# Channel tiles of the S5 heads ahead of the second half's token part, mixers' transfers issued by GpSimd, in a two-layer hybrid decoder trunk

## The chip, the core and the metric

One Trainium2 chip, one core. The engines are TensorE (PE), VectorE (DVE), ScalarE (ACT), GpSimd (POOL) and SyncE (SP); each works through its own stream of instructions in order, and streams meet at semaphores. A transfer is issued by one of the engines and carried out by the DMA engines. The metric is the device time of one execution in microseconds; a kernel's figure is the median of its runs.

## What is computed

Two layers over 1024 tokens of width 1024. In each layer one input projection feeds three kinds of heads, their normalised outputs are joined by an output projection, and then come a feed-forward block and a gate on a per-layer input embedding `p`:

```python
def hybrid_layer(h, p_i, cos, sin, ...):
    xn = rmsnorm(h, attn_norm_g)
    z = xn @ w_in
    za, zq, zk, zv, zc = jnp.split(z, [...], axis=-1)
    ya = chunk_gmlp(za, gmlp_ln_g, gmlp_ln_b, gmlp_ws, gmlp_bs)
    q = apply_rope(rmsnorm(q, q_norm_g), cos, sin)
    k = apply_rope(rmsnorm(k, k_norm_g), cos, sin)
    yb = swa_sink_attention(q, k, v, sinks)
    yc = s5_ssm(zc, ...)
    y = jnp.concatenate([rmsnorm(ya, ...), rmsnorm(yb, ...), rmsnorm(yc, ...)], axis=-1)
    h = h + y @ w_out
    hn = rmsnorm(h, mlp_norm_g)
    h = h + jnp.square(jax.nn.relu(hn @ w_ff1)) @ w_ff2
    gate = jax.nn.sigmoid(rmsnorm(h, ple_norm_g) @ w_ple_gate)
    return h + gate * (p_i @ w_ple_proj)
```

## The kernel before

**Tiling.** The tokens are cut into two halves of 512 (`h` = 0, 1). Every fp32 product is three fp32r matmuls of high and low parts, so a weight tile is loaded (`st`), rounded by ScalarE (line 104) and its remainder taken by VectorE (line 105) before TensorE uses it. PSUM has banks by tag: two `mm`, two `s`, and one each of `p`, `o`, `x`, `t`. An accumulation group of 24 matmuls of 512 columns fills a bank.

**First phase (to about 300 us).** `project0` makes layer 0's input projection for both halves. `z_tok(l, h, part)` has tokens on partitions: part 0 gives gmlp's gate half, k and v (stored to DRAM as `zg`), part 1 gives q (`zq`); each is 96 matmuls into four banks and four evictions, in which ScalarE writes a `z` tile from pool `zs` (two buffers) and a transfer stores it. `z_chan(l, h, m)` has channels on partitions: tiles m = 0, 1 feed S5 (`zu`), 2, 3 gmlp (`za`). Before, the order is z_tok of half 0 (part 0, 1), of half 1 (part 1 with the kept weights, then part 0), then the eight channel tiles. `embed` transposes `p` and multiplies it by `w_ple_proj` for both layers; its tiles `ptk` and `pjz` come from `zs` too, and `pjz` is stored as `pj`. Beside that, `ssm_tables` and `ssm_prep` compute S5's rotation tables (`tc_`, `ts_`, by doubling) and kernels (`kt`, `gq`, `pe`), stored as `par1`, `par2`, which `ssm` loads as `p1`, `p2` with `u` from `zu`. `psS` in the trace is S5's matmul of states (line 845), `pk`, `pq` and `pss` are attention's transposes and scores.

**Main phase.** `mix_out(0, 0)` is the output projection of half 0 (input tiles 0, 1 from gmlp, 2 to 5 attention, 6, 7 S5; its first three output tiles are begun on six input tiles). Then four `window`s run (feed-forward, gate), with the mixers of the following half as side lanes: `left_lane` carries S5 and attention of both halves of layer 0, `mix_lane` those of layer 1. Lanes are generators that are advanced at rates, with flags between them (`wait`); the scheduler sets the final order of each engine's stream from the program so written.

**Queues.** Before, all 855 transfers are issued by SP, weights and mixers' loads and stores in one stream, in order. POOL computes the rotation tables (36 operations, `cmul` with the engine `self.G`), clears `xp`, and does a few set-up instructions.

Of the kernel before, what the change touches and what calls it, by code (L numbers as in the profile page):

```python
# [62 lines left out]
class Trunk:  # L63


    def __init__(self, tc, ctx, a):
        self.tc, self.ctx, self.a = tc, ctx, a
        self.nc = nc = tc.nc
        self.V, self.S, self.G, self.T, self.Q = nc.vector, nc.scalar, nc.gpsimd, nc.tensor, nc.sync
        self.lanes, self.nbank, self.flags = [], 0, set()  # L70
        self.X, self.R, self.H, self.hst = {}, {}, {}, {}

# [290 lines left out]
    def setup(self):  # L363
# [4 lines left out]
        self.zs = self.pool(self.ctx, "zs", 2)  # L368
        self.xy = self.pool(self.ctx, "xy")
# [134 lines left out]
    def ssm_tables(self, t):  # L504
# [6 lines left out]
        for i, nm in enumerate(("ssm_a_re", "ssm_a_im")):  # L511
            Q.dma_start(rows[0:N, i, :], a[nm].rearrange("l (j e) p -> (l j) (e p)", e=2))
        Q.dma_start(ldr, a["ssm_log_dt"].rearrange("l (j e) -> (l j) e", e=2))
# [76 lines left out]
        for n in (1, 2, 4, 8, 16, 32):  # L590
# [3 lines left out]
                      bc(tc_), bc(ts_), tq[:, :, 0:n], self.G)  # L594
        for l in range(DEPTH):
            for gh in range(2):
                c = slice(l * 8 + gh * 4, l * 8 + gh * 4 + 4)
                for i, x in enumerate((tc_, ts_, r0)):
                    Q.dma_start(self.par1[l][gh][:, 1024 + i * 260:1284 + i * 260],
                                x[:, c, :].rearrange("p j b -> p (j b)"))  # L600

    def ssm_prep(self, l, t, tag, nb):

        a, V, S, G, T, Q = self.a, self.V, self.S, self.G, self.T, self.Q
        for gh in range(2):
# [3 lines left out]
            for x, nm in ((br, "ssm_b_re"), (bi, "ssm_b_im")):  # L609
                Q.dma_start(x, a[nm][l, gh * 8:gh * 8 + 8].rearrange("(j e) p h -> (e p) j h", e=2))  # L610
# [9 lines left out]
            for x, nm in ((cr, "ssm_c_re"), (ci, "ssm_c_im")):  # L620
                cl = t.tile([P, 2, 64], F32, name="cl", bufs=2)
                src = a[nm][l, gh * 8:gh * 8 + 8].rearrange("g h p -> (g h) p")
                Q.dma_start(cl[:, 0, :], src)
                Q.dma_start(cl[:, 1, :], src)
# [22 lines left out]
            Q.dma_start(self.par1[l][gh][:, 0:1024], pe.rearrange("p r j c -> p (r j c)"))  # L647
# [4 lines left out]
            for ri in range(2):  # L652
                Q.dma_start(self.par2[l][gh][:, ri * 512:(ri + 1) * 512].rearrange("p (j c) -> p j c", j=4),
# [5 lines left out]
            Q.dma_start(dk, a["ssm_d"][l, gh * 8:gh * 8 + 8].rearrange("(j e) h -> (e h) j", e=2))  # L659
# [25 lines left out]
    def z_tok(self, l, h, part, weights, ss):  # L685
# [13 lines left out]
        pss = [self.bank(tag) for tag in ("s", "s", "p", "o")]  # L699
# [13 lines left out]

    def z_sums(self):
# [36 lines left out]
    def project0(self):  # L751
# [18 lines left out]
        self.z_roots(0, 1, ss)  # L770
# [8 lines left out]
    def embed(self):  # L779
# [21 lines left out]
        for l in range(DEPTH):  # L801
            for i in range(2):
                w = F.next()
                for n in range(8):
                    h, m = n // 4, n % 4
                    ps, z = self.bank("mm"), self.zs.tile([P, 512], F32, tag="z", name="pjz")
# [3 lines left out]
                    Q.dma_start(self.pj[l][h][4 * i + m], z)  # L810
# [7 lines left out]
    def ssm(self, l, h, side, tag="p"):  # L818
# [706 lines left out]
```

## Time and profile before

| | |
|---|---|
| runs | 2393.14, 2386.28, 2385.95 us |
| median | 2386.28 us |
| profiled execution, its own time | 2391.88 us |
| its span | 2390.2 us |
| PE busy | 2327.5 us (97%) |
| VectorE, ScalarE, GpSimd busy | 1551.3, 1029.1, 33.5 us |
| granted clock over the span | 0.989 |
| transfers | 294.07 MB, 41.0% of 16 DMA engines |

PE is the engine on which the time stands, so the profile is read for PE's gaps: where they lie, what released PE after each, and what that releaser was waiting for in its turn. The granted clock is a share of TensorE's full 2.4 GHz.

### The profile page before, as it was taken

The numbers are of one execution on the slowest core, as the hardware profiler recorded it, in microseconds if no ns is written. First come the engines' busy times: TensorE is split into PE (matmuls) and PEld (weight loads), VectorE is DVE, ScalarE is ACT, GpSimd is POOL, SyncE is SP. The second block draws the span as 40 slices with busy tenths as digits, with TensorE's granted clock in tenths as the row PEclk, the third lists the DMA queues.
The fourth block names the chain that finished last, engine by engine and source line by source line (L and its number), as shares of the span: only waits on it lengthen the run. The fifth ranks groups of instructions, "written<-read, shape, count | busy, mean of one in ns | idle before, by whom it ended". The sixth has DMA issues, their size and how long they took to land.

```text
span 2390.2 us, 29266 instructions
## 1 busy us (share of the span) xinstructions
PE 2327.5 (97%) x10941; PEld 1885.4 (79%) x10941; DVE 1551.3 (65%) x2664; ACT 1029.1 (43%) x1787; POOL 33.5 (1%) x51
## 2 busy tenths in 40 slices
PE   7998999999999999999999999999999999999998
PEld 5777777788788887777888888777888887888887
DVE  7777678675966765576585774676757674444455
ACT  7355646433434443553342543464334343322333
POOL 0400000000000000000000000000000000000000
PEclk9999999999999999999999999999999999999999
DMA  8555542253553345324443344422534434333333
GB/s 246 175 153 171 175 127 75 80 164 100 154 154 104 110 129 144 103 71 141 128 134 115 106 136 132 137 76 80 164 105 136 123 93 137 97 92 95 96 97 98
DMA packets 403559, 295.95 MB, mean 124 GB/s; under 512 B 66668, under 2 KB 376024, under 8 KB 401624
## 3 DMA queue, kind: packets, MB, share of 16 engines
q1 hardware_dynamic: 403416, 294.07, 41.0%
q8 instruction: 86, 1.41, 0.2%
q14 instruction: 57, 0.47, 0.1%
HBM read 250.48 MB, written 43.54 MB: 123 GB/s over the span
## 4 chain that ended last, share of the span: by engine, by line
PE 82%; DMA 6%; DVE 4%; ACT 2%; issue 1%; SPq 0%; ACTq 0%; DVEq 0%
PE mm_ps L356 44%; PE x_ps L356 20%; PE s_ps L356 8%; DMA st<-in_w_in 2%; DVE w L105 2%; ACT w L104 1%; PE po L1242 1%; PE pss L1184 1%; PE p_ps L356 1%; DMA st<-in_w_out 1%; DMA pj<-pjz 1%; PE p_ps L931 1%; PE s_ps L706 1%; PE pt L1221 1%; PE psY L888 1%
## 5 line engine op out<-in xcount | busy, mean ns | idle before, releaser
L104 ACT CAST w<-st 128x1024 fp32r<-128x1024 f32 x364 | 387.4, 1067 | 844.0 <-PE mm_ps L356 438.1
L356 PE MATMUL mm_ps<-x,w 128*128 128x512 f32 x2904 | 711.3, 397 | 8.6 <-ACT pjz L809 4.1
L356 PEld LDWEIGHTS mm_ps<-x,w 128*128 128x128 f32 x2904 | 547.0, 190 | 135.4 <-issue 11.7
L105 DVE TENSOR_TENSOR w<-st,w 128x1024 fp32r<-128x1024 f32 x364 | 448.8, 1235 | 201.8 <-ACT w L104 196.1
L356 PE MATMUL mm_ps<-A,w 128*128 128x512 f32 x2016 | 500.9, 392 | 1.3 <-DVE H L1317 1.3
L356 PEld LDWEIGHTS mm_ps<-A,w 128*128 128x128 f32 x2016 | 376.0, 188 | 84.0 <-DVE H L1317 3.3
L356 PE MATMUL x_ps<-A,w 128*128 128x512 f32 x1056 | 273.5, 393 | 4.1 <-DVE H L1317 4.1
L356 PE MATMUL x_ps<-x,w 128*128 128x512 f32 x1104 | 272.0, 393 | 0.0
L356 PE MATMUL s_ps<-x,w 128*128 128x512 f32 x1056 | 251.8, 390 | 4.4 <-DVE w L105 2.7
L356 PEld LDWEIGHTS x_ps<-x,w 128*128 128x128 f32 x1104 | 205.7, 188 | 45.6 <-issue 3.4
L356 PEld LDWEIGHTS x_ps<-A,w 128*128 128x128 f32 x1056 | 196.3, 188 | 50.7 <-DVE H L1317 8.3
L356 PEld LDWEIGHTS s_ps<-x,w 128*128 128x128 f32 x1056 | 197.8, 188 | 48.6 <-DVE w L105 4.0
L1317 DVE TENSOR_TENSOR H<-H,mm_ps 128x512 f32<-128x512 f32 x168 | 113.3, 684 | 85.0 <-PE mm_ps L356 84.3
L1328 DVE SCALAR_TENSOR_TENSOR r<-mm_ps,rbc 128x512 f32<-128x512 f32 x88 | 60.7, 689 | 116.8 <-PE mm_ps L356 116.6
L706 PE MATMUL s_ps<-w,x 128*128 128x512 f32 x384 | 101.3, 403 | 3.9 <-ACT x L89 2.0
L1317 DVE TENSOR_TENSOR H<-H,x_ps 128x512 f32<-128x512 f32 x88 | 60.2, 684 | 67.8 <-PE x_ps L356 67.2
L1332 DVE TENSOR_TENSOR A<-q,A 128x512 fp32r<-128x512 f32 x128 | 87.7, 685 | 7.1 <-ACT q L1331 6.9
L706 PEld LDWEIGHTS s_ps<-w,x 128*128 128x128 f32 x384 | 73.3, 194 | 21.3 <-ACT x L89 2.4
L1330 ACT ACTIVATE A<-r 128x512 fp32r<-128x512 f32 x128 | 80.2, 626 | 6.9 <-DVE r L1328 6.9
L1331 ACT ACTIVATE q<-r 128x512 f32<-128x512 f32 x128 | 78.9, 617 | 0.0
L1207 ACT ACTIVATE pr<-pr,anm,hf 128x128 f32<-128x128 f32 x128 | 61.6, 483 | 20.1 <-DVE anm L1204 20.1
L90 DVE SCALAR_TENSOR_TENSOR x<-H,gT,x 128x512 fp32r<-128x512 f32 x80 | 57.4, 746 | 1.4 <-ACT x L89 1.4
(381 smaller groups left out, 2130.6 us busy)
## 6 DMA issues: line engine op xcount, KB each, us to landing
st<-in_w_ff SPq DMA_DIRECT2D x256, 512.0 KB, 4.1
st<-in_w_out SPq DMA_DIRECT2D x32, 512.0 KB, 4.1
st<-in_w_ple_gate SPq DMA_DIRECT2D x32, 512.0 KB, 4.1
st<-in_w_in SPq DMA_DIRECT2D x18, 512.0 KB, 4.5
p<-par SPq DMA_DIRECT2D x8, 1024.0 KB, 6.9
pj<-pjz SPq DMA_DIRECT2D x32, 256.0 KB, 2.0
H<-hs SPq DMA_DIRECT2D x4, 2048.0 KB, 8.7
pj<-pj SPq DMA_DIRECT2D x32, 256.0 KB, 3.6
```

Of the source, the lines that this page charges most:

```text
L90: self.V.scalar_tensor_tensor(lo, x, g, hi.bitcast(F32), ALU.mult, ALU.subtract)
L104: self.S.copy(hi, src)
L105: self.V.tensor_tensor(lo, src, hi.bitcast(F32), ALU.subtract)
L356: self.T.matmul(ps, w[:, i, k, c0:c0 + P], X[:, j, k, :], start=(start and n == 0), stop=(stop and n == last))
L706: T.matmul(pss[b], X[:, j, 2 * s + kk, c], w[:, i, kk, :], start=(s == 0 and kk == 0 and n == 0), stop=(s == 3 and kk == 1 and n == 2))
L888: T.matmul(psY[:, j], gqm[:, ri, j, :], xp[:, ri, j], start=(ri == 0), stop=False)
L1207: S.activation(pr[:, i], pr[:, i], AF.Exp, bias=nm[:, i:i + 1], scale=f[:, i:i + 1], accum_out=den[:, i:i + 1])
L1317: V.tensor_tensor(H[:, m], H[:, m], ps, ALU.add)
L1328: V.scalar_tensor_tensor(r, ps, 0.0, self.R[h][1], ALU.max, ALU.mult)
L1330: S.activation(A[:, 0, m], r, AF.Square)
L1331: S.activation(q, r, AF.Square)
L1332: V.tensor_tensor(A[:, 1, m], q, A.bitcast(F32)[:, 0, m], ALU.subtract)
```

## The change

It has four parts. (1) The S5 channel tiles (m = 0, 1, both halves) stand in `project0` before part 0 of half 1, the weight plan follows, and a flag `("zu", 0, 0)` lets S5 of half 0 start when they are done; `ssm` waits for `("z", l, h)` before it writes its output into X. Part 1 of half 1 goes to banks mm, mm, s, s and part 0 to p, o, s, s. (2) The rotation tables are computed by VectorE. (3) A pool `pz` adds two `z` buffers once both parts of `z_tok` are done for both halves, for `z_chan` 2, 3 and `embed`, and is closed before `mix_out(0, 0)`. gmlp and attention of half 0 start behind that point (flag `zg` in place of `zw`), and attention of half 1 waits for `("h", 0, 0)`, the end of `mix_out(0, 0)`, in place of a flag set inside it. (4) 351 transfers are issued by POOL: all loads and stores of the mixers, the stores of `z`, the loads of `ptk`, the stores of `pj`, the tables and kernels of S5. 520 stay on SP: weights, x, `hs`, `H`, the loads of `pj`, the output. The transfers of `zu` and `yt` are cut in two halves of 64 partitions, 16 more.

```diff
 def main_plan(self):
...
+        chan = self.z_chan_plan(0)
+        yield next(chan)
+        yield next(chan)
         yield from self.z_tok_plan(0, 0)
-        yield from self.z_chan_plan(0)
+        yield from chan
...
 def ssm_tables(self, t):
...
             self.cmul(tc_[:, :, n + 1:2 * n + 1], ts_[:, :, n + 1:2 * n + 1], tc_[:, :, 1:n + 1], ts_[:, :, 1:n + 1],
-                      bc(tc_), bc(ts_), tq[:, :, 0:n], self.G)
+                      bc(tc_), bc(ts_), tq[:, :, 0:n])
...
-                    Q.dma_start(self.par1[l][gh][:, 1024 + i * 260:1284 + i * 260],
+                    self.G.dma_start(self.par1[l][gh][:, 1024 + i * 260:1284 + i * 260],
...
-    def z_tok(self, l, h, part, weights, ss):
+    def z_tok(self, l, h, part, weights, ss, tags=("s", "s", "p", "o")):
...
-            z = self.zs.tile([P, 512], F32, tag="z", name="z")
+            z = self.zt()
             S.activation(z, ps, AF.Copy, scale=sc)
-            Q.dma_start((self.zq if part else self.zg)[l][h][b], z)
+            self.G.dma_start((self.zq if part else self.zg)[l][h][b], z)
...
-        pss = [self.bank(tag) for tag in ("s", "s", "p", "o")]
+        pss = [self.bank(tag) for tag in tags]
...
+    def zt(self, name="z"):
+
+        self.nz += 1
+        pools = self.zpools
+        return pools[self.nz % len(pools)].tile([P, 512], F32, tag="z", name=name)
...
 def z_chan(self, l, h, m, w, tag):
...
-            Q.dma_start(self.zu[l][h][m].rearrange("s p b -> p s b"), zv)
+            for r in (slice(0, 64), slice(64, P)):
+                self.G.dma_start(self.zu[l][h][m][:, r].rearrange("s p b -> p s b"), zv[r])
...
 def project0(self):
...
-        yield from self.z_tok(0, 1, 1, lambda s: kept[s], ss)
-        self.flags.add("zw")
-        yield
-        yield from self.z_tok(0, 1, 0, lambda s: F.next(), ss)
+        yield from self.z_tok(0, 1, 1, lambda s: kept[s], ss, ("mm", "mm", "s", "s"))
+
+        def chan(ms):
+            for m in ms:
+                w = F.next()
+                for h in range(2):
+                    yield from self.z_chan(0, h, m, w, "mm")
+
+        yield from chan((0, 1))
+        self.flags.add(("zu", 0, 0))
+        yield from self.z_tok(0, 1, 0, lambda s: F.next(), ss, ("p", "o", "s", "s"))
         self.z_roots(0, 1, ss)
-        for m in range(4):
-            w = F.next()
-            for h in range(2):
-                yield from self.z_chan(0, h, m, w, "mm")
+        self.flags.add("zg")
+        yield
+        yield from chan((2, 3))
...
 def embed(self):
...
-                    ps, z = self.bank("mm"), self.zs.tile([P, 512], F32, tag="z", name="pjz")
+                    ps, z = self.bank("mm"), self.zt("pjz")
...
-                    Q.dma_start(self.pj[l][h][4 * i + m], z)
+                    self.G.dma_start(self.pj[l][h][4 * i + m], z)
...
 def left_lane(self):
...
-        yield from self.wait(("z", 0, 0))
+        yield from self.wait(("zu", 0, 0))
         yield from self.ssm(0, 0, 1, "x")
...
-        yield from self.wait("early")
+        yield from self.wait(("h", 0, 0))
         yield from self.attention(0, 1, 1)
...
 def run(self):
...
-        self.until(lambda: "zw" in self.flags)
+        self.until(lambda: {"zg", "rotary"} <= self.flags)
         zws.close()
-        self.until(lambda: "rotary" in self.flags)
         self.lanes.remove(z0)
+        pzs = ExitStack()
+        self.zpools.append(self.pool(pzs, "pz", 2, side=self.side(0), reuse_waits="tile"))
         self.lane(self.gmlp(0, 0, 0, "x", [("attn", 0, 0)]), RATE0)
...
         self.until(lambda: {("attn", 0, 0), ("gm", 0, 0)} <= self.flags)
+        self.zpools.pop()
+        pzs.close()
```

The lines left out turn the other `Q.dma_start` of the mixers and S5's preparation into `self.G.dma_start`, and take one name for a tile.

How the streams move, at three places. First the transfers. Before, this is SP's stream where it stores the first half's q (`zq_146`) and S5's tables (`par_113` to `par_116` are `par1` of the two layers and group halves, `par_117`, `par_118` two of `par2`):

```order
L599 DMA par_113<-tc__644 128x260
...
L647 DMA par_113<-pe 128x1024
...
L599 DMA par_113<-ts__645 128x260
...
L694 DMA zq_146<-z 128x512 x2
L681 DMA par_117<-kt 16x4x128 x16
L694 DMA zq_146<-z 128x512
```

Now the same transfers in POOL's stream, from the first store of q on:

```order
L698 DMA zq_146<-z 128x512
L685 DMA par_117<-kt 16x4x128 x16
L698 DMA zq_146<-z 128x512
L603 DMA par_113<-tc__644 128x260
...
L603 DMA par_116<-ts__645 128x260
L698 DMA zq_146<-z 128x512
L657 DMA par_118<-gq 128x4x128 x2
L698 DMA zq_146<-z 128x512
L651 DMA par_114<-pe 128x1024
L685 DMA par_118<-kt 16x4x128 x16
L698 DMA zq_147<-z 128x512 x2
```

The sixteen `kt` stores moved ahead of the second store of q, eight table stores stand between the second and the third, and the second `kt` group ahead of the fifth. Farther down the same stream of POOL, up to the load of S5's input `u`:

```order
L841 MEMSET xp 128x1024
L848 DMA p_1502<-par_113 128x1804
L850 DMA p_1504<-par_117 128x2048
L698 DMA zq_147<-z 128x512 x2
L992 DMA lng<-in_gmlp_ln_g 128x256
L992 DMA lnb<-in_gmlp_ln_b 128x256
L1134 DMA q<-zq_146 128x512
L744 DMA zu_122<-z 64x8x64 x2
L744 DMA zu_124<-z 64x8x64 x2
L1134 DMA q<-zq_146 128x512
L846 DMA u<-zu_122 128x512
```

The last two stores of the second half's q now stand behind the mixers' first loads, and the load of `u` comes 72 transfers after the first store of q.

Second, PE behind part 1 of half 1 (`x_222` and `x_447` are the normalised inputs of half 0 and 1). Before, from the end of that token projection:

```order
L706 MATMUL p_ps<-w,x_447 128x512 x6
L706 MATMUL o_ps<-w,x_447 128x512 x4
L1103 MATMUL pk<-identr,kst 128x128 x4
L706 MATMUL o_ps<-w,x_447 128x512 x2
L356 MATMUL mm_ps<-x_222,w 128x512 x23
L1103 MATMUL pk<-identr,kst 128x128 x4
L356 MATMUL mm_ps<-x_222,w 128x512
L356 MATMUL mm_ps<-x_447,w 128x512 x24
L1103 MATMUL pk<-identr,kst 128x128 x4
L1171 MATMUL pq<-identr,qst 128x128 x4
L1184 MATMUL pss<-kT,qt 128x128 x8
```

Now, from the last matmuls of part 1 (banks mm, s), and its continuation at the end of part 0:

```order
L710 MATMUL mm_ps<-w,x_447 128x512 x12
L710 MATMUL s_ps<-w,x_447 128x512 x12
L710 MATMUL p_ps<-w,x_447 128x512 x6
L710 MATMUL o_ps<-w,x_447 128x512 x5
L359 MATMUL mm_ps<-x_222,w 128x512 x24
L359 MATMUL mm_ps<-x_447,w 128x512 x24
...
L710 MATMUL s_ps<-w,x_447 128x512 x24
...
L710 MATMUL s_ps<-w,x_447 128x512 x10
L1122 MATMUL pk<-identr,kst 128x128 x8
L359 MATMUL mm_ps<-x_222,w 128x512 x24
L359 MATMUL mm_ps<-x_447,w 128x512 x24
L862 MATMUL psS<-u,p_1502 64x64 x16
```

Two S5 channel tiles moved between the first eleven matmuls of part 0 and the rest, the other two stand behind it, and S5's states follow at once; attention's first transposes stand behind part 0 instead of inside it.

Third, PE at the end of `embed` and the start of `mix_out(0, 0)`. Before (`y_1996` is S5's output before its gate, `ssq` its sum of squares, `os` attention's, `va` gmlp's; `x_2068` is the embedding, `x_1992` the joined input of the output projection):

```order
L285 MATMUL t_ps<-os,onesr 128x256
L931 MATMUL x_ps<-y_1996,gw 128x512 x6
L356 MATMUL mm_ps<-x_2068,w 128x512 x12
L931 MATMUL x_ps<-y_1996,gw 128x512 x6
L356 MATMUL mm_ps<-x_2068,w 128x512 x6
L931 MATMUL x_ps<-y_1996,gw 128x512 x6
L356 MATMUL mm_ps<-x_2068,w 128x512 x12
L285 MATMUL x_ps<-ssq,onesr 128x512
L356 MATMUL mm_ps<-x_2068,w 128x512 x6
L356 MATMUL mm_ps<-x_1992,w 128x512 x36
L356 MATMUL s_ps<-x_1992,w 128x512 x18
```

Now (`x_2246` the embedding, `x_2176` the joined input):

```order
L359 MATMUL mm_ps<-x_2246,w 128x512 x4
L1261 MATMUL po<-pp,v 64x256 x2
L359 MATMUL mm_ps<-x_2246,w 128x512 x2
L1261 MATMUL po<-pc,vd 64x256 x2
L359 MATMUL mm_ps<-x_2246,w 128x512 x12
L288 MATMUL x_ps<-va,onesr 128x512
L288 MATMUL t_ps<-os,onesr 128x256
L359 MATMUL mm_ps<-x_2246,w 128x512 x18
L359 MATMUL mm_ps<-x_2176,w 128x512 x4
L359 MATMUL s_ps<-x_2176,w 128x512 x2
```

The roots of gmlp (`va`) and attention (`os`) now stand last, with 18 embedding matmuls behind them; S5's root moved up.

## Rows read from the trace of the kernel before

**Rows 1.** The page, part 4: the chain that ended last, by engine.

```profile
PE 82%; DMA 6%; DVE 4%; ACT 2%; issue 1%; SPq 0%; ACTq 0%; DVEq 0%
```

**Rows 2.** Windows: length, busy us (instructions) per engine, granted clock, DMA share, GB/s.

```profile
0.00:400.00 400.00, 360.51 (x1788) 286.89 (x1788) 294.59 (x714) 229.20 (x507) 31.54 (x49) 0.96 0.54 164
400.00:2391.00 1991.00, 1966.97 (x9154) 1598.53 (x9153) 1256.68 (x1951) 799.86 (x1282) 1.92 (x2) 1.00 0.39 116
```

**Rows 3.** Windows around gaps; columns as above: PE, PEld, DVE, ACT, POOL.

```profile
80.00:100.00 20.00, 15.65 (x68) 12.33 (x67) 11.78 (x33) 1.82 (x3) 4.93 (x4) 0.91 0.46 146
140.00:160.00 20.00, 17.18 (x77) 14.57 (x76) 15.30 (x43) 7.84 (x18) 0.00 (x0) 0.83 0.72 193
190.00:220.00 30.00, 23.41 (x177) 18.58 (x178) 25.59 (x65) 19.61 (x51) 0.00 (x0) 0.89 0.59 192
280.00:300.00 20.00, 16.29 (x58) 12.49 (x57) 9.50 (x15) 7.23 (x14) 0.00 (x0) 0.83 0.40 138
310.00:330.00 20.00, 15.96 (x69) 12.55 (x70) 18.14 (x32) 10.31 (x16) 0.00 (x0) 1.00 0.56 157
360.00:380.00 20.00, 17.39 (x87) 15.28 (x86) 16.92 (x36) 13.79 (x38) 0.00 (x0) 0.83 0.30 92
930.00:980.00 50.00, 44.56 (x191) 35.57 (x192) 30.61 (x52) 17.70 (x29) 0.00 (x0) 0.97 0.55 152
```

**Rows 4.** PE's timeline: start, length, what, in brackets idle before and releaser.

```profile
76.07 3.23 PE L706 MATMUL s_ps<-w,x 128*128 128x512 f32 x13 [0.25 <-DVE hss L697]
...
92.67 4.61 PE L706 MATMUL o_ps<-w,x 128*128 128x512 f32 x12 [4.35 <-DVE hss L697]
...
285.69 5.49 PE L356 MATMUL mm_ps<-x,w 128*128 128x512 f32 x12 [3.71 <-ACT pjz L809]
```

**Rows 5.** SP's issue timeline, 72 to 97 us: start, length, transfers issued.

```profile
72.74 0.33 SPq L694 DMA_DIRECT2D zq<-z  x1
...
82.01 0.79 SPq L599 DMA_DIRECT2D par<-tc__644  x2
...
87.97 0.95 SPq L694 DMA_DIRECT2D zq<-z  x2
89.02 7.49 SPq L681 DMA_DIRECT2D par<-kt  x16
```

**Rows 6.** ScalarE's timeline at the fourth eviction of the first half's q.

```profile
90.65 0.69 ACT L693 ACTIVATE z<-o_ps,rtm 128x512 f32<-128x512 f32 x1 [8.88 <-DMA zq<-z]
```

**Rows 7.** SP's issue timeline near the end of the embedding.

```profile
273.33 0.37 SPq L1276 DMA_DIRECT2D H<-hs  x1
```

**Rows 8.** The chain that ended last, in order of time: start, length, what.

```profile
273.92 11.06 DMA pj<-pjz
...
478.29 10.88 PE mm_ps L356 x48
```

**Rows 9.** gmlp's root in half 0: PE's first matmul, VectorE's last step.

```profile
257.60 1.02 PE L285 MATMUL x_ps<-va,onesr 128*128 128x512 f32 x2
...
271.86 1.41 DVE L90 SCALAR_TENSOR_TENSOR x<-u,gT,x 128x512 fp32r<-128x512 f32 x2
```

**Rows 10.** POOL's instructions by form: count, busy us, mean ns, idle before.

```profile
L824 POOL MEMSET xp<- 128x1024 f32 x4 | 3.8, 956 | 1506.5 <-DVE or L294 706.1 <-DVE rt L1126 489.7 <-ACT pr L1207 280.2
L256 POOL TENSOR_TENSOR tc__644<-tc__644,tq 128x512 f32<-128x512 f32 x1 | 1.6, 1638 | 0.0
...
L255 POOL TENSOR_TENSOR tq<-ts__645 128x64 f32<-128x64 f32 x1 | 1.4, 1373 | 0.1
...
L254 POOL TENSOR_TENSOR tc__644<-tc__644 128x64 f32<-128x64 f32 x1 | 0.3, 303 | 0.0
```

**Rows 11.** Transfers by issue: engine, count, KB each, median us to landing.

```profile
zq<-z SPq DMA_DIRECT2D x16, 256.0 KB, 2.1
...
u<-zu SPq DMA_DIRECT2D x8, 256.0 KB, 3.5
```

**Rows 12.** VectorE's timeline: a product of 512 elements a row.

```profile
54.61 0.69 DVE L254 TENSOR_TENSOR pw<-lr,bbr 128x512 f32<-128x512 f32 x1
```

More of the change, by code (lines that the diff above doesn't have):

```diff
@@ L69, in __init__ @@
         self.V, self.S, self.G, self.T, self.Q = nc.vector, nc.scalar, nc.gpsimd, nc.tensor, nc.sync
-        self.lanes, self.nbank, self.flags = [], 0, set()
+        self.lanes, self.nbank, self.nz, self.flags = [], 0, 0, set()
         self.X, self.R, self.H, self.hst = {}, {}, {}, {}
@@ L368, in setup @@
         self.zs = self.pool(self.ctx, "zs", 2)
+        self.zpools = [self.zs]
         self.xy = self.pool(self.ctx, "xy")
@@ L511, in ssm_tables @@
         for i, nm in enumerate(("ssm_a_re", "ssm_a_im")):
-            Q.dma_start(rows[0:N, i, :], a[nm].rearrange("l (j e) p -> (l j) (e p)", e=2))
-        Q.dma_start(ldr, a["ssm_log_dt"].rearrange("l (j e) -> (l j) e", e=2))
+            self.G.dma_start(rows[0:N, i, :], a[nm].rearrange("l (j e) p -> (l j) (e p)", e=2))
+        self.G.dma_start(ldr, a["ssm_log_dt"].rearrange("l (j e) -> (l j) e", e=2))
         yield
@@ L622, in ssm_prep @@
                 src = a[nm][l, gh * 8:gh * 8 + 8].rearrange("g h p -> (g h) p")
-                Q.dma_start(cl[:, 0, :], src)
-                Q.dma_start(cl[:, 1, :], src)
+                self.G.dma_start(cl[:, 0, :], src)
+                self.G.dma_start(cl[:, 1, :], src)
                 pc = self.ps.tile([P, 512], F32, tag=tag, name="pc")
@@ L726, in z_chan @@
         V, Q, bc = self.V, self.Q, self.R[h][1]
-        ps, z = self.bank(tag), self.zs.tile([P, 512], F32, tag="z", name="z")
+        ps, z = self.bank(tag), self.zt()
         yield from self.cm(ps, w, 0, self.X[h], range(NK))
@@ L787, in embed @@
                 for b in range(2):
-                    t = self.zs.tile([P, 512], F32, tag="z", name="ptk")
+                    t = self.zt("ptk")
                     r = (4 * h + 2 * b) * P
-                    Q.dma_start(t.rearrange("p (b c) -> p b c", b=2),
+                    self.G.dma_start(t.rearrange("p (b c) -> p b c", b=2),
                                 a["p"][l, 0, r:r + 2 * P, :].rearrange("(b p) c -> p b c", p=P))
@@ L828, in load @@
             u = sp.tile([P, 8, 64], F32, name="u")
-            Q.dma_start(u.rearrange("p g b -> p (g b)"), zu[gh].rearrange("s (h g) b -> (s h) (g b)", g=8))
+            self.G.dma_start(u.rearrange("p g b -> p (g b)"), zu[gh].rearrange("s (h g) b -> (s h) (g b)", g=8))
             p1 = sp.tile([P, 1804], F32, name="p1")
-            Q.dma_start(p1, self.par1[l][gh])
+            self.G.dma_start(p1, self.par1[l][gh])
             p2 = sp.tile([P, 2048], F32, name="p2")
-            Q.dma_start(p2, self.par2[l][gh])
+            self.G.dma_start(p2, self.par2[l][gh])
             st[gh] = [u, p1, p2]
@@ L891, in outputs @@
             S.copy(ye, psY)
-            Q.dma_start(yu[gh].rearrange("t (h g) b -> (t h) (g b)", g=8), ye.rearrange("p j e b -> p (j e b)"))
+            self.G.dma_start(yu[gh].rearrange("t (h g) b -> (t h) (g b)", g=8), ye.rearrange("p j e b -> p (j e b)"))
             yt = sp.tile([P, 512], F32, tag="yt", name="yt")
-            Q.dma_start(yt.rearrange("p (t b) -> p t b", t=8), yu[gh].rearrange("t p b -> p t b"))
+            for r in (slice(0, 64), slice(64, P)):
+                self.G.dma_start(yt[r].rearrange("p (t b) -> p t b", t=8), yu[gh][:, r].rearrange("t p b -> p t b"))
             st[gh].append(yt)
@@ L944, in ssm @@
         yield
+        yield from self.wait(("z", l, h))
         X = self.X[h]
@@ L961, in gmlp @@
         va = gm.tile([P, 4, 256], F32, name="va")
[L962 removed]
+        self.G.dma_start(va, self.zg[l][h][:, :, 0:256].rearrange("b p c -> p b c"))
         u = gm.tile([P, 2, 512], F32, name="u")
[L964 removed]
+        self.G.dma_start(u, self.za[l][h])
         wl = gm.tile([P, 4, P], F32, name="wl")
[L966 removed]
+        self.G.dma_start(wl, a["gmlp_ws"][l].rearrange("a p c -> p a c"))
         bsb = gm.tile([P, 2, P], F32, name="bsb")
         for hh in range(4):
[L969 removed]
+            self.G.dma_start(bsb[(hh % 2) * 64:(hh % 2) * 64 + 64, hh // 2, :], a["gmlp_bs"][l, hh].partition_broadcast(64))
         lng = gm.tile([P, 256], F32, name="lng")
@@ L972, in gmlp @@
         for x, nm in ((lng, "gmlp_ln_g"), (lnb, "gmlp_ln_b")):
[L973 removed]
+            self.G.dma_start(x, a[nm][l].rearrange("a b -> (a b)").partition_broadcast(P))
         yield
@@ L1285, in mix_out @@
             yield from self.wait(("ssm", l, h))
-            self.flags.add("early")
         for m in range(NK):
```

29 lines of the change are left out of this document (12 added, 17 removed).

## The prediction

> **What bounds the kernel now.** I began with the chain of waits [rows 1]: TensorE (PE) makes 82% of the chain that ended last, so a change that leaves its matmuls as they are (and this one does) can only move the gaps between them and the clock. The windows say where the gaps are [rows 2]: in the first 400 us PE is busy 360.51, so 39.5 us are idle at a mean clock of 0.96; in the 1991 us behind, 24.0 are idle at 1.00. More than half of what can be won lies in the first sixth of the span, which is where the change is. A finer table [rows 3] has the spots: idle us, plus the length times what the clock lacks of 1.00. They are 80 to 100 (4.35 + 1.8 = 6.2), 140 to 160 (2.8 + 3.4 = 6.2), 190 to 220 (6.6 + 3.3 = 9.9), 280 to 300 (3.7 + 3.4 = 7.1), 310 to 330 (4.0), 360 to 380 (2.6 + 3.4 = 6.0), 930 to 980 (5.4 + 1.5 = 6.9): 46.3 in all. Where the clock falls, PE had a gap just before: the 4.35 us gap ends at 92.67 [rows 4], and the window around it has 0.91.
>
> Then the queue of transfers on SyncE (SP), because two of the gaps end there. At 80 to 100 [rows 5] the first eviction store zq<-z leaves at 72.74, but the next two only at 87.97, behind eight transfers of the rotation tables that GpSimd (POOL) is computing until then, the first of which leave at 82.01. ScalarE (ACT), with two z buffers, sits 8.88 us before its next eviction [rows 6], and PE waits for the o bank. At 273.33 the 2 MB load H<-hs is issued [rows 7], a store pj<-pjz behind it takes 11.06 us on the chain [rows 8], and PE waits 3.71 us for pjz at 285.69 [rows 4].
>
> **The change part by part.** The sum is made against the profiled execution (2391.88 us, span 2390.2), which lies 5.6 us above the median of 2386.28; I carry that difference unchanged and subtract from the median. About 0.3%, 7.2 us, is what a measurement of this kernel tells from no change.
>
> Gains. (1) 80 to 100: the stores no longer stand behind transfers that wait for the tables, and the second half's first part uses banks mm, mm, s, s, so PE doesn't need the o bank there. I take 6 of 6.2. (2) 140 to 160: attention started amid token projection; by the order it now starts behind it, with channel tiles beside it. I take 5 of 6.2, since the waits for kT and qt are its own. (3) 190 to 220 and 280 to 300, embedding: four z buffers instead of two let a load or store be two tiles late, and the stores pj<-pjz leave the queue that carries H and the weights. I take 14 of 17.0. (4) 310 to 330: the waits here are casts and the residual sum; weights are freer on SP. 2 of 4.0. (5) 360 to 380, second half's attention: the softmax chain stays. 3 of 6.0. (6) 930 to 980, with weight loads on SP no longer behind mixers' loads: 4 of 6.9. Sum 34; the bounds are 0 and 46.3.
>
> Cost 1, the end of the first phase. Before, S5's root came last and 54 early matmuls of the output projection followed it. Now gmlp's root is last, with 18 embedding matmuls behind it, and the output projection's first input tile is gmlp's. From that root's matmul (257.60) to the end of the tiles that it yields (271.86 + 1.41) took 15.7 us [rows 9]. A 512-column matmul takes 10.88/48 = 0.227 us [rows 8], so 18 of them cover 4.1; 11.6 are bare, and I add 3.4 us of clock, the loss beside the 3.71 us gap (280 to 300). 15.0 us. From below it is 0 if lanes run sooner than the order suggests.
>
> Cost 2, GpSimd as issuer. 351 transfers move to it, in one queue in a fixed order. No row of before shows what it takes GpSimd to issue one. SP took 7.49/16 = 0.47 us for a kt store [rows 5], the cheap end; GpSimd's dearest instruction was 1.64 us [rows 10], the dear end. I take 0.956 us, its memset: an instruction that reads no tensor, as a descriptor list does not, though it is far from the same thing. Call the price p. By the order, behind the first zq store (at about 76, where PE starts the second half, [rows 4]) stand 16 kt stores, zq store 2, eight table stores, zq store 3 (26th), store 4 (29th), 16 more kt stores, store 5 (47th), and as the 72nd the load of u. With two z buffers, eviction n waits for store n-2. PE starts the second half at 76.07; 96 matmuls and some 2 us of small ones end at about 100; after 11 more it wants the mm bank of eviction 5 (102.5), after 48 + 13 more the s bank of eviction 7 (116.4), after 72 more, the k transposes (1.1) and 48 more the states' u (144.7). A store lands in 2.1 us, u in 3.5 [rows 11], an eviction is 0.69 [rows 6]. Lateness: mm 26p - 23.7, s 47p - 37.6, u (with the memset of 0.96) 72p - 64.2. At 0.47 all are negative: nothing. At 0.956 they are 1.2, 7.3 and 4.6, and the largest counts: 7.3 us. At 1.64 it is 53.9. Behind that come loads with slack: at 0.956 the queue is idle most of the time (351 x 0.956 = 336 of 2390 us).
>
> The Trainium skill (SBUF — State Buffer, section "SBUF: two separate sides") speaks against this move: descriptors of a GpSimd-issued transfer are written by GpSimd itself, and while VectorE holds the port pair that the two share they can't be; it gives about 620 ns alone and 3100 ns beside a copy on VectorE. By 3.1 us cost 2 would be, as an estimate, 72 x 3.1 - 64.2 = 159 us. No run here shows a transfer from GpSimd.
>
> Tables on VectorE: 36 operations, from 512 elements a row (0.69 us, [rows 12]) down to 16, about 10 us in all. VectorE has 105 us free in the first 400 [rows 2], so I take 0; without that cover at most 10. Split zu and yt transfers, 16 more issues: in p. Reordered weights: the two S5 tiles need their weights earlier, and the same casts run. 0.
>
> Sum: 34 - 15.0 - 7.3 = 11.7 us; 2386.3 - 11.7 = 2374.6, say 2375.
>
> **The rivals.** (a) GpSimd's queue becomes the bound, slower. Mechanism: in-order issue from 76 to 165 us holds z buffers, then banks, then u. Nothing else changed, it pays from cost 2 = 19.2, that is p = 1.16 (72p = 83.4); slower by over 0.3% from p = 1.26. Speaking for it: GpSimd's instructions stretch while VectorE works; two products of the same 64 elements took 303 and 1373 ns [rows 10], and VectorE is busy 74% of the first 400 us [rows 2]. A mean of 1.45 gives 40.2 us, 2386.3 - 34 + 15 + 40.2 = 2407.5; 1.64 gives 2421. Against it: a memset of 131,072 elements costs less than 1 us.
>
> (b) Nearly even. The gaps at 280 to 300, 360 to 380 and 930 to 980 are the transfers themselves, not their queue; then 7, 3 and 4 of the gains fall away and 34 - 14 - 22.3 = -2.3 remains: 2388.6; with half of them, 2381.6. The Trainium skill (DMA: Bandwidth & Descriptors, "Issuing engines are not separate DMA queues") says just that: all issuers feed the same 16 engines, and only issue time is saved. Against it: pj<-pjz took 11.06 us behind H, against 2.1 for an equally large zq store [rows 8, 11].
>
> (c) All gaps close and issuing is as cheap as SP's: 46.3 - 15.0 = 31.3, 2355. For it: the order already pushes what hangs on stores behind other work. Against it: chains of ACT and VectorE own part of each gap.
>
> (d) The change doesn't do what it says, the transfers staying where they were: 2386. The order has them on POOL, so 1 in 50, counted in (b).
>
> **How the numbers follow.** Forecast 0.45 (p from 0.8 to 1.05, 2367 to 2379), (a) 0.27, (b) with (d) 0.20, (c) 0.08. Faster is forecast and (c): 0.53; same is (b): 0.20; slower is (a): 0.27. The likeliest single time is 2375. The range goes from somewhat beyond (c), 2350, to (a) at 1.45, 2408; above it lies about a third of (a), below it a small part of (c), some 0.12 together.
>
> **What would show it.** Right: GpSimd's queue shows transfers at 0.8 to 1.05 us each; no gap of over 2 us for the o bank near 92; PE waits some 7 us between 100 and 130 for a bank whose eviction waits for zq<-z; the gap before the output projection (270 to 300) names gmlp's x or a reciprocal root, with a clock under 0.9 behind it; pj<-pjz lands in about 2 us although H is loading. Wrong: a price over 1.2, or issue time that grows with the shape (kt against u), makes (a); a last gap under 5 us refutes cost 1 and brings 2365; PE gaps with the same releasers at 360 and 930 as before make (b). What I trust least is p, then cost 1.

## The result, and the profile after

The changed kernel takes 2429.29 us (median of 4 runs, 2428.27 to 2433.6) beside 2386.42 before: a ratio of 1.0175 (95% interval 1.016 to 1.019), 43 us slower. 2375 was predicted, with a range of 2350 to 2408. The profiled execution took 2433.6 us, its span is 2431.9.

The page, part 4 (chain by engine) and part 3 (queues: packets, MB, share), then windows as in [rows 2]:

```profile
PE 73%; issue 5%; DVE 3%; DMA 3%; ACT 1%; POOL 0%; ACTq 0%; POOLq 0%; DVEq 0%
```

```profile
q1 hardware_dynamic: 332984, 224.49, 31.1%
q0 software_dynamic: 21792, 69.58, 9.1%
```

```profile
0.00:400.00 400.00, 337.52 (x1633) 269.58 (x1634) 273.97 (x691) 204.27 (x441) 104.16 (x190) 0.91 0.54 160
400.00:2431.00 2031.00, 1998.33 (x9310) 1621.18 (x9308) 1285.44 (x2011) 822.25 (x1346) 103.05 (x177) 1.00 0.38 114
```

Against [rows 2] PE is busy 23 us less in the first 400 us, at a clock of 0.91 instead of 0.96; and on the chain PE fell from 82% to 73%, while "issue", a wait for nothing that the profile shows, came up to 5%. Transfers of 69.58 MB now run in a second queue.

A good mark for the end of the first phase is VectorE's first step of the first window, the same operation in both kernels:

```profile
370.72 0.69 DVE L1328 SCALAR_TENSOR_TENSOR r<-mm_ps,rbc 128x512 f32<-128x512 f32 x1
```

```profile
393.64 0.69 DVE L1346 SCALAR_TENSOR_TENSOR r<-mm_ps,rbc 128x512 f32<-128x512 f32 x1
```

The first row is of before, the second of after: 22.9 us are lost by then, and another 19 by the last such step (2311.60 and 2353.48). This mark is used for all runs below. Of the 41.7 us by which the span grew, PE is idle for 33.3; its instructions, equal in number, take the other 8.4 (busy 2335.8 instead of 2327.5).

**Where PE waits now.** PE's timeline of after, its three longest gaps in the first phase (in brackets idle before, and releaser):

```profile
152.96 1.12 PE L1122 MATMUL pk<-identr,kst 128*128 128x128 f32 x4 [7.85 <-DVE kst L1119]
```

```profile
213.93 0.69 PE L812 MATMUL mm_ps<-identr,ptk 128*128 128x128 f32 x2 [7.98 <-DVE z L746]
```

```profile
320.14 2.08 PE L359 MATMUL mm_ps<-x,w 128*128 128x512 f32 x4 [8.46 <-ACT x L89]
```

The gap for the o bank of [rows 4] is gone, and so is the 3.71 us for pjz. The third gap is the tail of cost 1. The first two are new, and both lead back to GpSimd's stream. Its timeline in after, 76 to 132 us:

```profile
76.53 8.32 POOL L685 DMA_DIRECT2D par<-kt  x16 [8.41 <-DVE bd L671]
...
113.86 0.79 POOL L1070 DMA_DIRECT2D k<-zg  x1
118.06 0.76 POOL L1070 DMA_DIRECT2D v<-zg  x1 [3.41 <-issue]
...
121.81 0.77 POOL L981 DMA_DIRECT2D va<-zg  x1 [1.40 <-issue]
126.91 0.75 POOL L985 DMA_DIRECT2D wl<-in_gmlp_ws  x1 [4.33 <-issue]
...
130.66 0.57 POOL L848 DMA_DIRECT2D p<-par  x1
131.31 0.54 POOL L850 DMA_DIRECT2D p<-par  x1
```

A piece is a run of elements that lie side by side in one partition: a `kt` store has four on each of 16 partitions, 64 in all, and the load of `k` four on each of 128, 512 in all. An issue costs 8.32/16 = 0.52 us for a `kt` store and 0.79 us for `k`. But behind `k` GpSimd does nothing for 3.41 us before it issues `v`, and 4.33 before `wl`, with no releaser. `k`, `v` and `va` land 3.8, 3.4 and 4.7 us after their issue, at 117.7, 121.5 and 126.5, and each time the next transfer of 512 pieces leaves 0.3 to 0.4 us later. It looks as if GpSimd waited until the one ahead had drained. Over the whole run GpSimd's longest waits put down to "issue" (us in all, times, longest; the group named is the one that waited) are, but for `graw` (128 pieces), those of transfers of 512 pieces:

```profile
POOL zu L744 <- issue: 23.2, 10, 3.0
POOL graw L935 <- issue: 16.8, 3, 10.6
POOL yt L912 <- issue: 16.4, 5, 4.6
POOL v L1070 <- issue: 14.3, 4, 3.8
POOL wl L985 <- issue: 13.5, 3, 5.2
```

From there to PE's first gap: 9.1 us of such waits (3.41 + 1.40 + 4.33) push S5's two 1 MB loads of `par` to 130.66, and then SP's weight loads, ScalarE and VectorE are late in turn. SP's issues from 125 us, ScalarE's and VectorE's next weight steps:

```profile
125.37 1.92 SPq L98 DMA_DIRECT2D st<-in_w_in  x4
...
134.41 7.96 SPq L98 DMA_DIRECT2D st<-in_w_in  x3
```

```profile
145.94 1.04 ACT L104 CAST w<-st 128x1024 fp32r<-128x1024 f32 x1 [7.14 <-DMA st<-in_w_in]
```

```profile
147.01 1.22 DVE L105 TENSOR_TENSOR w<-st,w 128x1024 fp32r<-128x1024 f32 x1 [7.50 <-ACT w L104]
```

Three issues take 7.96 us where four took 1.92 just before, the cast waits 7.14 for its weights, and VectorE, which works in order, computes `kst` (what PE waits for) only behind that. That the `par` loads are what slowed the weight loads is inferred from the times; ring_double below moves the `par` loads forward, and PE's gap shrinks.

The second gap is shorter to follow. GpSimd, ScalarE and VectorE of after around 207 us:

```profile
202.45 0.73 POOL L912 DMA_DIRECT2D yt<-yu  x1 [3.96 <-DMA yu<-ye]
207.37 0.70 POOL L912 DMA_DIRECT2D yt<-yu  x1 [4.19 <-issue]
```

```profile
210.23 0.63 ACT L212 ACTIVATE gelu_t<-yt 128x512 f32<-128x512 f32 x1 [9.23 <-DMA yt<-yu]
```

```profile
210.89 0.69 DVE L213 SCALAR_TENSOR_TENSOR gelu_t<-gelu_t,yt 128x512 f32<-128x512 f32 x1 [6.68 <-ACT gelu_t L212]
```

The second half of `yt` leaves 4.19 us late, ScalarE waits 9.23 for it (the rest is the first half's wait for `yu` and the landing), VectorE 6.68 for ScalarE, and the eviction `z` for which PE waits stands behind that in VectorE's stream.

### The profile page after: what moved, and what is told of

Same layout as the page of the kernel before. It is cut to its first block, busy times and chain, and to the rows that moved or that the text cites. A ratio compares the mean times of both kernels' runs of the same rounds, so it can differ in the third digit from the quotient of the medians.

```text
span 2431.9 us, 29416 instructions
## 1 busy us (share of the span) xinstructions
PE 2335.8 (96%) x10941; PEld 1890.8 (78%) x10941; DVE 1559.4 (64%) x2700; ACT 1026.5 (42%) x1787; POOL 207.2 (9%) x366
## 3 DMA queue, kind: packets, MB, share of 16 engines
q0 software_dynamic: 21792, 69.58, 9.1%
## 4 chain that ended last, share of the span: by engine, by line
PE 73%; issue 5%; DVE 3%; DMA 3%; ACT 1%; POOL 0%; ACTq 0%; POOLq 0%; DVEq 0%
PE mm_ps L359 39%; PE x_ps L359 18%; PE s_ps L359 8%; PE po L1261 1%; PE p_ps L359 1%; DMA st<-in_w_in 1%; DVE w L105 1%; PE pss L1203 1%; ACT w L104 1%; PE p_ps L949 1%; PE pt L1240 1%; PE pq L1190 0%; DMA st<-in_w_out 0%; DVE H L1335 0%; PE psY L905 0%
## 5 line engine op out<-in xcount | busy, mean ns | idle before, releaser
L105 DVE TENSOR_TENSOR w<-st,w 128x1024 fp32r<-128x1024 f32 x364 | 448.8, 1234 | 222.7 <-ACT w L104 217.8
L1346 DVE SCALAR_TENSOR_TENSOR r<-x_ps,rbc 128x512 f32<-128x512 f32 x40 | 27.6, 689 | 59.2 <-PE x_ps L359 59.0
```

The lines of the kernel that those rows point to most:

```text
L105: self.V.tensor_tensor(lo, src, hi.bitcast(F32), ALU.subtract)
L1346: V.scalar_tensor_tensor(r, ps, 0.0, self.R[h][1], ALU.max, ALU.mult)
```

## The experiments

Each run was measured beside the kernel before on one chip; not all runs were on the same chip, and the kernel before took 2386.4 to 2390.1 us on them, so two runs compare best by their ratios. Theory A is that the loss comes with GpSimd as issuer; theory B that it comes from the early S5 tiles, which hold a weight buffer. "Mark" is the start of the first window (370.7 before, 393.6 after).

| run | median us | ratio to before (95%) | mark |
|---|---|---|---|
| after_all_sp | 2383.89 | 0.9984 (0.9973 to 0.9994) | 362.2 |
| before_pool | 2412.09 | 1.0109 (1.0086 to 1.0132) | 373.8 |
| after_late_chan | 2431.44 | 1.0187 (1.0163 to 1.0211) | 392.0 |
| after_pieces_sp | 2400.63 | 1.0053 (1.0033 to 1.0074) | 372.9 |
| one_buffer | 2464.73 | 1.0314 (1.0295 to 1.0333) | 396.2 |
| ring_double | 2432.39 | 1.0183 (1.0163 to 1.0203) | 377.3 |
| ring_late | 2440.91 | 1.0231 (1.0209 to 1.0253) | 377.1 |
| sp_late_chan | 2380.86 | 0.9959 (0.9945 to 0.9974) | 357.0 |
| sp_pj_pool | 2385.83 | 0.9986 (0.9974 to 0.9998) | 367.2 |
| sp_late_tab_pool | 2392.34 | 1.0028 (1.0015 to 1.0041) | 373.9 |
| sp_late_two_z | 2392.81 | 1.0022 (1.0012 to 1.0032) | 370.1 |
| sp_late_early | 2379.39 | 0.9963 (0.9949 to 0.9976) | 359.2 |

### Issuer or S5 tiles?

**after_all_sp**: the change with every `self.G.dma_start` turned back.

```diff
-            self.G.dma_start((self.zq if part else self.zg)[l][h][b], z)
+            self.Q.dma_start((self.zq if part else self.zg)[l][h][b], z)
...
```

> The changed kernel with every transfer issued by SP again; early S5 tiles, tables on VectorE and the extra z buffers stay. By the order the second S5 channel tile then directly follows the first, instead of standing behind the whole part 0. Theory A (the loss comes with GpSimd's queue, by its own delays or by the order that it brings): 2370 to 2390 us, SP's 48 us wait for a weight buffer near 77 us is gone and so is the 7.85 us gap at 153. Theory B (the loss comes from the early S5 tiles holding a weight buffer, whoever issues): over 2405 us, with a wait of SP for a weight buffer of over 30 us between 75 and 130.

2383.89: the whole loss of 43 us is gone, and 0.16% more. PE is busy 363.68 us of the first 400, at a clock of 0.97:

```profile
0.00:400.00 400.00, 363.68 (x1814) 290.96 (x1814) 299.54 (x753) 227.17 (x503) 3.46 (x13) 0.97 0.55 165
```

**before_pool**: the kernel before, with the same transfers on GpSimd.

```diff
-            Q.dma_start((self.zq if part else self.zg)[l][h][b], z)
+            self.G.dma_start((self.zq if part else self.zg)[l][h][b], z)
...
```

> The kernel before with the mixers' transfers issued by GpSimd and the zu and yt transfers in halves, nothing else of the change; the rotation tables stay on GpSimd and share its stream. Theory A: 2410 to 2430 us, most of the loss. Theory B: within 8 us of 2386, since no S5 tile moved.

2412.09, 1.1% slower, in theory A's range. Its mark is only 3.0 us late, but the last such step is 19.2 us late: the main phase loses 16 us by GpSimd issuing, as in the change (19). In the first phase GpSimd stands still as long here as in the change (its waits put down to "issue" before 400 us add up to 49 us, in the change to 46), yet that costs 3 us here and 31 in the changed program (393.6 against 362.2 in after_all_sp). So the waits alone are not the loss; it needs an order in which work that PE wants soon stands behind them. Which part of the change brings that order was not separated; the next run excludes the S5 tiles.

**after_late_chan**: the change with the S5 tiles back behind part 0.

```diff
-        yield from chan((0, 1))
-        self.flags.add(("zu", 0, 0))
         yield from self.z_tok(0, 1, 0, lambda s: F.next(), ss, ("p", "o", "s", "s"))
         self.z_roots(0, 1, ss)
         self.flags.add("zg")
         yield
+        yield from chan((0, 1))
+        self.flags.add(("zu", 0, 0))
         yield from chan((2, 3))
```

> The changed kernel with the S5 channel tiles back behind part 0 of the second half, with GpSimd issuing as in the change. Theory B: 2390 to 2405 us, the gap at 145 to 153 (7.85 us, clock 0.68) gone. Theory A: over 2415 us, since GpSimd still issues.

(The two lines `yield next(chan)` of the weight plan go too.) 2431.44, as slow as the change. Theory B falls: with GpSimd issuing, moving the tiles back wins nothing.

### Why GpSimd is slow

**after_pieces_sp**: seven kinds of transfers back on SP, all made of several pieces a partition.

```diff
-                self.G.dma_start(self.zu[l][h][m][:, r].rearrange("s p b -> p s b"), zv[r])
+                self.Q.dma_start(self.zu[l][h][m][:, r].rearrange("s p b -> p s b"), zv[r])
...
-        self.G.dma_start(va, self.zg[l][h][:, :, 0:256].rearrange("b p c -> p b c"))
+        self.Q.dma_start(va, self.zg[l][h][:, :, 0:256].rearrange("b p c -> p b c"))
...
```

> The changed kernel with only those transfers back on SP that are made of four to eight pieces a partition (zu, yt, k, v, va, wl, the embedding's loads): in the trace of the change GpSimd sits 2 to 4.5 us behind each of them with no releaser shown. If that sitting is what costs (theory A, its own delays): 2390 to 2405 us, and the 8 us gap at 214 is gone. If it is the order or the S5 tiles: over 2415 us.

2400.63: 29 of the 43 us return, two thirds, with 60 of the 351 transfers moved. The scheduler also made a new order for this program (PE's differs from 133 us on), so by itself the run doesn't tell the waits from the order; the next pair does.

**one_buffer** and **ring_double** share one edit that frees memory; ring_double then doubles the memory that holds descriptors of GpSimd's transfers (the list of pieces that the DMA engines work through). Up to about 870 us all engines have the same order in both.

```diff
-        pr = at.tile([P, 4, P], F32, name="pr", bufs=2)
+        pr = at.tile([P, 4, P], F32, name="pr", bufs=1)
...
-    nc = bacc.Bacc("TRN2", target_bir_lowering=False, num_devices=1, dynamic_dma_scratch_size=1024)
+    nc = bacc.Bacc("TRN2", target_bir_lowering=False, num_devices=1, dynamic_dma_scratch_size=2048)
```

(The second pair is in ring_double alone.)

> A control: the changed kernel with one buffer instead of two for attention's probabilities, which frees 2 KB a partition and orders attention more tightly. No theory speaks of that buffer; the time is expected within 15 us of the change, 2415 to 2445. It is there to be compared with ring_double, which has the same edit.

> The same as one_buffer, with twice the memory for the descriptors of GpSimd's transfers (2048 in place of 1024 bytes a partition). The order of all engines is the same through the first phase and most of layer 0. Theory A1 (GpSimd sits behind a transfer of many pieces because the memory for its descriptors is full until earlier transfers have drained): the waits of 2 to 4.5 us behind k, va and zu shrink to under 1 us where two such transfers follow one another, and the time falls by 15 to 30 us against one_buffer. Theory A2 (GpSimd's own work on many pieces, or the scheduler's order): the same waits, and within 5 us of one_buffer.

One_buffer takes 2464.73, dearer than expected (its loss against the change, 33 us by the last window step, arises behind 1240 us, where PE waits 8.66 us for `gt` at 1446.97 and again at 2031.88), so its use is as the control. Ring_double takes 2432.39, 32 us less. It has the same two waits for `gt`, which the change has not, so that its time near the change's says nothing against the larger memory. GpSimd's timeline, first of one_buffer, then of ring_double:

```profile
114.33 0.79 POOL L1070 DMA_DIRECT2D k<-zg  x1
118.40 0.76 POOL L1070 DMA_DIRECT2D v<-zg  x1 [3.28 <-issue]
...
122.05 0.77 POOL L981 DMA_DIRECT2D va<-zg  x1 [1.29 <-issue]
127.02 0.75 POOL L985 DMA_DIRECT2D wl<-in_gmlp_ws  x1 [4.21 <-issue]
...
130.78 0.57 POOL L848 DMA_DIRECT2D p<-par  x1
```

```profile
113.48 0.79 POOL L1070 DMA_DIRECT2D k<-zg  x1
114.26 0.76 POOL L1070 DMA_DIRECT2D v<-zg  x1
...
116.61 0.76 POOL L981 DMA_DIRECT2D va<-zg  x1
118.06 0.75 POOL L985 DMA_DIRECT2D wl<-in_gmlp_ws  x1 [0.69 <-issue]
...
122.51 0.57 POOL L848 DMA_DIRECT2D p<-par  x1
```

`v` now leaves 0.78 us behind `k`, the wait before `wl` is 0.69 instead of 4.21, and the load of `par` starts 8.3 us sooner. PE's gap follows, one_buffer above, ring_double below:

```profile
153.40 1.12 PE L1122 MATMUL pk<-identr,kst 128*128 128x128 f32 x4 [7.83 <-DVE kst L1119]
```

```profile
147.45 1.12 PE L1122 MATMUL pk<-identr,kst 128*128 128x128 f32 x4 [2.79 <-DVE kst L1119]
```

PE's second gap goes from 7.87 us (214.14, for `qt`) to 2.17 (197.18). Over the whole run GpSimd's waits put down to "issue" fall from 142.9 us in 42 to 18.0 in 7, of which `graw` has 10.2 and `k` 5.5. Those of `zu`, first of one_buffer:

```profile
POOL zu L744 <- issue: 23.7, 10, 3.0
```

```profile
POOL zu L744 <- issue: 0.9, 1, 0.9
```

The mark comes 18.9 us sooner (396.2 to 377.3) in the same order of instructions. So theory A1 is shown for the first phase: GpSimd holds its stream until descriptor memory is free, and a transfer of many pieces fills it. What the memory brings behind 870 us is mixed with another order.

**ring_late** joins ring_double with the late S5 tiles of after_late_chan (the two edits above).

> ring_double with the S5 channel tiles back behind part 0 of the second half, GpSimd issuing as in the change. It asks where the rest of the first phase's loss sits once GpSimd no longer waits for descriptor memory: ring_double starts its first window at 377.3 us, the kernels with all transfers on SP at 362.2 (S5 tiles early) and 357.0 (late). If the rest is the place that the early S5 tiles take when GpSimd issues (the second tile behind part 0, its weight in the ring), the first window starts at 357 to 365 and the time is 2412 to 2422; if it is GpSimd's serial issue and later landing, at 372 to 380 and 2427 to 2437.

The mark at 377.1 is that of the second expectation, but 2440.91 us lies above both ranges. It is 0.5% more than ring_double with the same mark, so this difference arises in the main phase; it wasn't traced. Even with most of the waits gone (ring_late has one of 9.08 us left, before `p` at 182.77), GpSimd as issuer ends the first phase 15 to 20 us behind the kernels on SP. Part of it is a longer tail, the gap for gmlp's root before the output projection:

```profile
304.19 2.08 PE L357 MATMUL mm_ps<-x,w 128*128 128x512 f32 x4 [10.80 <-ACT x L89]
```

It is 2.29 us in sp_late_chan, whose engines have another order (the scheduler makes a new one for every program). How much of the rest is order and how much the later landing of each store (3.3 us median for zq<-z in after, against [rows 11]) wasn't separated.

### What the other parts are worth

**sp_late_chan**: after_late_chan with all transfers on SP.

> The changed kernel with all transfers on SP and the S5 channel tiles back behind part 0: what is left are the tables on VectorE, the extra z buffers and the banks. If the early S5 tiles are worth something on their own, 2386 to 2392, some 3 to 8 us over the kernel with all transfers on SP (2383.9); if the gain of the first phase came from the tables and buffers, within 3 us of it.

2380.86 and a mark of 357.0, the earliest of all, as the second expectation had it: the S5 tiles ahead of part 0 bring nothing, if anything they cost (362.2 in after_all_sp). PE, first 400 us, and the gap at the tail:

```profile
0.00:400.00 400.00, 367.19 (x1833) 294.25 (x1834) 302.20 (x758) 229.65 (x511) 3.47 (x13) 0.97 0.55 166
```

```profile
284.75 1.20 PE L357 MATMUL mm_ps<-x,w 128*128 128x512 f32 x4 [2.29 <-ACT x L89]
```

**sp_pj_pool**: after_all_sp, with only the embedding's stores on GpSimd.

```diff
-                    Q.dma_start(self.pj[l][h][4 * i + m], z)
+                    self.G.dma_start(self.pj[l][h][4 * i + m], z)
```

> All transfers on SP except the 32 stores of the embedding (pj<-pjz, one piece of 2 KB a partition, so nothing to fill the memory of descriptors). If a second queue helps where SP's carries H and the weights, as the prediction held for 280 to 300, the waits for pjz (1.2, 1.4 and 1.0 us with all transfers on SP) go and the time falls by 3 to 6 us below 2383.9; if the transfers and not the queue set their time, it stays within 3 us.

2385.83 against 2383.89, intervals that overlap: no gain. PE's waits for pjz are 4.4 us in total (3 of them) against 3.6 with all transfers on SP:

```profile
PE mm_ps L359 <- ACT pjz L826: 4.4, 3, 2.0
```

```profile
PE mm_ps L359 <- ACT pjz L826: 3.6, 3, 1.4
```

**sp_late_tab_pool** is sp_late_chan with the rotation tables on GpSimd; **sp_late_two_z** is it without the pool `pz`; **sp_late_early** is it with the flag inside `mix_out` again.

```diff
-                      bc(tc_), bc(ts_), tq[:, :, 0:n])
+                      bc(tc_), bc(ts_), tq[:, :, 0:n], self.G)
```

```diff
-        self.zpools.append(self.pool(pzs, "pz", 2, side=self.side(0), reuse_waits="tile"))
...
-        self.zpools.pop()
-        pzs.close()
```

```diff
             yield from self.wait(("ssm", l, h))
+            self.flags.add("early")
...
-        yield from self.wait(("h", 0, 0))
+        yield from self.wait("early")
```

> sp_late_chan (all transfers on SP, S5 tiles behind part 0; 2380.9 us) with the rotation tables back on GpSimd. If the stores that wait for those tables were what cost near 90 us before (the prediction's first gain, 6 us), 2385 to 2389 with a gap of 3 to 5 us near 90 again; if the new banks (mm, mm, s, s) already absorb it, within 3 us of 2380.9.

2392.34, 0.7% over sp_late_chan, slower than expected. PE's gaps:

```profile
95.52 0.45 PE L628 MATMUL pc<-identr,cl 128*128 128x128 f32 x1 [4.32 <-issue]
...
300.08 2.07 PE L357 MATMUL mm_ps<-x,w 128*128 128x512 f32 x4 [14.20 <-ACT x L89]
```

And ScalarE's timeline just before the first:

```profile
91.01 0.69 ACT L695 ACTIVATE z<-o_ps,rtm 128x512 f32<-128x512 f32 x1 [9.31 <-DMA zq<-z]
```

The gap near 90 is back, as expected, and so is ScalarE's wait for a store of q ([rows 6] had 8.88), but the larger part is a tail of 14.20 us: its order again puts gmlp's root last. So the tables' place is worth about 4 us directly; the rest came with the order.

> sp_late_chan without the two extra z buffers. If they carry the gain in the embedding (the prediction's third gain, 14 us), 2387 to 2395, with waits for ptk and pjz back at 190 to 300; if not, within 3 us of 2380.9.

2392.81, 0.6% over sp_late_chan. Gaps for `z` and for the embedding's loads are back:

```profile
141.67 6.68 PE L357 MATMUL mm_ps<-x,w 128*128 128x512 f32 x21 [4.66 <-DVE z L740]
195.17 0.66 PE L810 MATMUL mm_ps<-identr,ptk 128*128 128x128 f32 x4 [2.59 <-DMA ptk<-in_p]
198.63 1.11 PE L810 MATMUL mm_ps<-identr,ptk 128*128 128x128 f32 x4 [2.23 <-DMA ptk<-in_p]
```

> sp_late_chan with attention of the second half waiting for the flag inside the first output projection again, as in the kernel before, instead of its end. If the later start costs (the gap of 2.6 us at 353), 2376 to 2379; if the earlier start takes VectorE from the residual sums there, as in the kernel before (gaps of 310 to 380), 2383 to 2387.

2379.39, not to be told from sp_late_chan, so neither of the expected moves. The start of the second half's attention costs or brings nothing that can be measured. Both beat the kernel before (by 0.4%) and the change.

## Why the prediction was wrong, point by point

- **What bounds the kernel** was right: PE's work is the same, and all of the 43 us are gaps and clock, 23 of them before the first window.
- **Cost 2, the step that failed.** It gave a transfer from GpSimd one price p, 0.956 us whatever its shape, and took rival (a) to begin at p = 1.16. It made 7.3 us; the measured cost of GpSimd's transfers is 45 (2429.29 against 2383.89). The issue itself costs 0.48 to 0.88 us, less than taken, by which cost 2 would have been nothing (47 x 0.54 - 37.6 and 72 x 0.54 - 64.2 are negative). PE's wait of some 7 us for a bank between 100 and 130 didn't come: its longest there is 0.91. What counted was a wait that the sum didn't have: GpSimd stands still until descriptor memory is free, for 1.4 to 5.2 us before `v`, `va`, `wl`, `zu` or `yt`. Doubling that memory brought the mark 18.9 us forward, moving seven kinds of such transfers back brought 29 us in all. The other 15 us by which the first phase stays behind after_all_sp (377.3 against 362.2) are open. "Issue time that grows with the shape" stood among the signs of being wrong, but was in no term and no bound. What u waited for was off too: its load was issued at 165.57, for want of the tiles `zu`, four of which left 2.9 us apart.
- **Beyond 400 us** the forecast let the queue be idle most of the time, and so free. It was idle, and yet before_pool and the change lose 16 and 19 us there. After_pieces_sp loses 6.3, so most of it again goes with the many-piece transfers, though in another order: a queue that is idle on the whole can still stall where such transfers come together. PE's waits of over 2 us behind 400 us are 2.67 (at 954.71), 3.02 (1524.47) and 2.27 (1578.49) in the change, against one of 2.87 (970.10) before. The rest lies in smaller waits and the clock and wasn't traced.
- **Rival (a)** named the right side and the right queue, with 2407 to 2421, and an in-order stream that holds back what stands behind it did show. What it built on, a price of over 1.16 us because GpSimd's instructions stretch beside VectorE, did not: `kt` stores average 0.515 us in the whole run with VectorE 68% busy in the first 400 us (273.97/400). The 3.1 us a transfer that the Trainium skill gives beside copies on VectorE (SBUF — State Buffer, section "SBUF: two separate sides") were not met, no issue taking over 0.88: the costliest group of VectorE on the page, 448.8 of 1559.4 us at line 105, is an operation on two tensors and not a copy.
- **Cost 1** was about right: 11.6 us of bare tail and 3.4 of clock were taken; PE waits 8.46 us at 320.14, and 0.59 before the 18 embedding matmuls, and by the prediction's measure the clock (0.86 and 0.88 in the windows 300 to 320 and 320 to 340) adds 5.2. It is a matter of the order, though: the gap is 2.29 with all transfers on SP and late S5 tiles, 14.20 with the tables on GpSimd.
- **Gains** were too large as well: 34 us, 19 net of cost 1. Without GpSimd's transfers the kernel gains 0.16% (after_all_sp) to 0.4% (sp_late_chan), about 4 to 10 us. Taking out the extra buffers loses 12 us (2392.81 against 2380.86), near the 14 of the third gain; taking out the tables about as much, though mostly through the order. Each is more than the whole gain, so the parts don't add up. The S5 tiles bring nothing. Gains 5 and 6 didn't come in the change: PE waits 4.12 us at 389.90 and 2.67 at 954.71, where before it waited 1.88 at 366.31 and 2.87 at 970.10.
- **pj<-pjz behind H.** The 11.06 us on the chain before were read as a queue's cost. A queue of its own for those stores brought nothing (sp_pj_pool). That is what rival (b) said. The Trainium skill (DMA: Bandwidth & Descriptors, "Issuing engines are not separate DMA queues") says the same, that several issuers save only the time of issuing, and this run agrees, with 2385.83 against 2383.89.

## What to carry to other kernels

Before transfers are moved to another issuer, count their pieces as well as their number: here a queue whose descriptors had to fit into 1024 bytes a partition stalled behind transfers of 512 pieces, and everything in that in-order stream stalled with it, stores that free buffers included. What such a stall costs depends on what stands behind it: 3 us in the first phase of the old order, 31 in that of the new. A wait in the chain on a transfer behind a large load is no proof that the queue is at fault. And where a scheduler re-orders each program, test parts in both directions, since a part's effect (the tables here) may come through the order it brings.

## What was not expected of the hardware

GpSimd issued a transfer in 0.51 us (`kt`, 64 pieces) to 0.79 us (`k`, 512), at the low end hardly more than SP's 0.47 for `kt` [rows 5]. Once its descriptor memory was full it waited until the transfer ahead had landed: `k` took 3.8 us to land, and `v` left 0.4 us after that; with twice the memory the same wait was nil. Landing came later from GpSimd for zq<-z: 3.3 us against 2.1 from SP [rows 11], but 2.5 with all transfers on SP in the changed program, so that part of the difference isn't the issuer's. For u<-zu it came sooner, 2.9 against 3.5.
